# Order of loads and stores at the start of the second SwiGLU product, and the engine of the last scaling

## The chip, the cores and the metric

The kernel runs on one core of a Trainium2 chip. The metric is the device time of one execution in microseconds (us). The core has five engines with a queue each: TensorE (PE; its weight loads are shown apart as PEld), VectorE (DVE), ScalarE (ACT), GpSimd (POOL) and SyncE (SP), which here issues nearly all DMAs, in the order in which the program emits them.

## The reference

One inference step of a two-layer decoder trunk with width 1024, for a prompt of 1024 positions and 8 samples of 4 positions, 1056 columns in all. Layer 0 mixes tokens by sliding-window attention, layer 1 by a recurrent block. After each mixer comes a SwiGLU with 2816 features, and at the end an RMS norm:

```
def swiglu(h, w_in, w_out):
    g, u = jnp.split(h @ w_in, 2, axis=-1)
    return (jax.nn.silu(g) * u) @ w_out

for layer in range(DEPTH):
    ...
    xp = xp + swiglu(rms_norm(xp, ffn_norm[layer]), w_ffn_in[layer], w_ffn_out[layer])
    xs = xs + swiglu(rms_norm(xs, ffn_norm[layer]), w_ffn_in[layer], w_ffn_out[layer])
y_prompt = rms_norm(xp, final_norm)
```

## The kernel before

**Tiles.** The columns lie in three tiles of 384, 384 and 288 (t = 0, 1, 2). A matrix of 1024 rows is held as 8 blocks of 128 partitions. All products are done in three passes, of a high and a low part of each operand (`mm3`, L310): an operand is copied to the high part on ACT, and the low part is a subtraction on DVE.

**First product.** `ffn_phase` goes over 22 blocks of 128 features. The first two are plain. The other 20 go in pairs of items from `blocks(f)`: `seven` does tiles 0 and 1 by a Strassen-like scheme of seven half products per pair of feature blocks (operands B11, B21, B22 of the normed input `xn` and their sums T1 to T4), and `h_in` does tile 2. Each item ends in a `post` that computes the gated features on ACT and DVE and puts them aside in DRAM: `keep` copies a tile to a buffer `hi` (ACT, L891), subtracts it (DVE, L892) and stores both halves (SP, L893 and L894). There is one buffer `hi` of one tag and two of another, `xs`, used in turn; a buffer is free again when its store has landed. An odd block stores six tiles of tiles 0 and 1 (`keep_pair`), then one of tile 2. The residual x had been put aside in DRAM (`xd`) before, for room.

**Second product.** It runs over 5 chunks of 4 feature blocks, 4 units each, `unit(w, ws, o, mp, steps)`. A unit has nine operands per chunk (b11, t3, b21, t2, h0, h1, t4, t1, b22; loaded by `fetch`, L202) and 66 matmuls. Its products go into PSUM banks and are added on DVE to x in SBUF (`add`, L1014); a bank that is accumulated further waits for the add that reads it. `add` is pinned: on DVE it stands behind the instruction emitted just before it. A unit's weights come as one raw tile (`load`, L149; two raw buffers), which `parts` splits (ACT L134, DVE L135) and turns into sums on POOL (L155 to L158), which `sums` splits in turn. Unit u issues the load of unit u + 3 and the parts of unit u + 2; within the units both splits are pinned too.

**The seam.** The work around the last two blocks (`y` for NF - 2, `z` for NF - 1) is written out by hand in `lead`, lists of actions put between the items. In `drive` an item runs its `fn` (the matmuls), frees its buffers, prepares what it can, and then runs its `post` (the stores). Before, six operands are fetched ahead of y, and the reload of x (six half tiles, L965), three operands and the weight of unit 2 follow the post of the first item of z.

**Room.** Operands and x lie in slots: six of a pool `hp` that the T operands use until the last `seven`, and 18 general ones, of which six are free before y.

**Order.** PE and SP run in the order in which the program emits. ACT, DVE and POOL are ordered by a planner, with the order of emission as priority; `high_priority(60)` moves an instruction 60 places ahead.

**The end.** In layer 1, `h_out` adds the last two feature blocks tile by tile (L1026), `square` collects squares (ACT L365, DVE L366), `rms` turns their sum into a factor (PE L373, DVE, POOL L379), `spread` spreads it over the partitions (PE, and a copy on ACT, L399), and `final_steps` scales x and stores it. The scaling is one fused multiply on DVE that reads the factor from PSUM (L1386), or a pre-scaling on ACT (L1396) and a multiply on POOL (L1384). Tile 0 goes by DVE, tile 1 by ACT and POOL, tile 2 by DVE but for blocks 2 and 5.

Of the kernel before, what the change touches and what calls it, by code (L numbers as in the profile page):

```python
# [12 lines left out]
P = 128  # L13
# [16 lines left out]
NT = 3  # L30
# [7 lines left out]
NP0 = 1  # L38
PRI = 60
NSH = 4  # L40

VEC = {}
_o = 0
# [12 lines left out]
class Slots:  # L56
    def __init__(self, names):
        self.free = list(names)
# [149 lines left out]


class Item:  # L210
    def __init__(self, fn, needs=(), frees=None, order=None):
        self.fn, self.needs = fn, list(needs)
        self.order = self.needs if order is None else list(order)
        self.frees = self.needs if frees is None else list(frees)
        self.halves = [self]
# [36 lines left out]
class Kern:  # L252
# [33 lines left out]
    def drive(self, items):  # L286
        need = [w for it in items if isinstance(it, Item) for w in it.order]
        todo = self.todo = []
        for w in need:
            if w not in todo:  # L290
                todo.append(w)
        for it in items:
            if it is GAP:
                continue
            if not isinstance(it, Item):
                it()
            else:
                while any(w.t is None for w in it.needs):
                    assert todo.pop(0).prep(self)
                post = it.fn(*[w.t for w in it.needs])  # L300
                for w in it.frees:
                    w.free(self)
                while todo and todo[0].prep(self):
                    todo.pop(0)
                if post:
                    post()

# [532 lines left out]
    def ffn_phase(self, l, before, after):  # L840
# [116 lines left out]
            if j == 3:  # L957
                self.freeall(self.xt[0] + self.xt[1])

        def reload():  # L960
            for t in range(NT):
                self.xt[t] = [self.act_tile([P, 4, WMAX], F32, "x") for _ in range(2)]
            for i in range(2):
                for t in range(NT):
                    nc.sync.dma_start(self.xt[t][i][0][:, :, :WID[t]], self.xd[t][:, 4 * i:4 * i + 4, :])  # L965


        def seven(wg, wu, ws, f):
# [47 lines left out]
        def h_out(w0, w1, h, t, steps):  # L1016
            W = WID[t]
            ws = (w0, w1)
            for m in range(KB):
                ps = self.bank()  # L1020
                for c in range(2):
                    self.mm3(ps[:, :W], ws[c][:, 0, m * P:(m + 1) * P], ws[c][:, 1, m * P:(m + 1) * P],
                             h[:, c, 0, :W], h[:, c, 1, :W], c == 0, c == 1)
                x = self.xview(t, m)
                with tc.high_priority(PRI):
                    tt(x, ps[:, :W], x, OP.add)  # L1026
                if l == 1 or t < 2:
                    self.square(t, m)
                for fn in steps.get(m, ()):
                    fn()  # L1030

# [56 lines left out]
        def second():  # L1088

            O = [[Operand(lambda c=c, i=i: OD[c, i], WMAX if isinstance(i, str) else WID[2], pools)  # L1090
                  for i in ("b11", "t3", "b21", "t2", 0, 1, "t4", "t1", "b22")] for c in range(NCH)]
            M = [Mixed(I[f"wz{l}"][c, mp]) for c in range(NCH) for mp in range(4)]
            n = len(M)
            M += [Whole(I[f"wd{l}"][k]) for k in range(2)]
            H = [Operand(lambda t=t: HD_[t], WID[t], pools) for t in range(NT)]
            gate = Gate()

            def do(u, what):
                if u < len(M):
                    getattr(M[u], what)(self)  # L1100

            def fetch(c, i, j):
                for o in O[c][i:j]:
                    assert o.prep(self)

            def pin(on):
                self.pinned = on

            lead = [[lambda: fetch(0, 0, 6)], [lambda: do(0, "load")],
                    [lambda: do(0, "parts"), lambda: do(0, "sums"), lambda: do(1, "load")],  # L1110
                    [reload, lambda: fetch(0, 6, 9), lambda: do(1, "parts"), lambda: do(2, "load")], [lambda: pin(True)],
                    [lambda: pin(False)]]
            items = []
            for u in range(n):
                c, mp = divmod(u, 4)

                def s0(u=u, c=c, mp=mp):
                    if mp < 3 and c + 1 < NCH:
                        fetch(c + 1, 3 * mp, 3 * mp + 3)
                    if mp < 3 and c + 1 == NCH:  # L1120
                        assert H[mp].prep(self)
                    do(u + 1, "sums")
                    do(u + 3, "load")
                    gate.open = u == n - 1

                st = (s0, lambda u=u: do(u + 2, "parts"))
                p = [M[u].w, M[u].s]
                items.append(Item(lambda a, b, *y, mp=mp, st=st: unit(a, b, y, mp, st), p + O[c],
                                  p + (O[c] if mp == 3 else []), [gate]))
            w = [x.w for x in M[n:]]  # L1130
            steps = [{}, {2: n0[1:2], 5: n0[3:4]}, {1: n1[1:2], 4: n1[3:4]}]
            last = [Item(lambda a, b, h, t=t: h_out(a, b, h, t, steps[t]), w + [H[t]],
                         (w if t == 2 else []) + [H[t]], [gate]) for t in range(NT)]
            return lead, items, last
# [8 lines left out]
        for f in range(NPL, NF - 2):  # L1143
            L += blocks(f)
        y, z = blocks(NF - 2), blocks(NF - 1)
        L += lead[0] + [y[0]] + lead[1] + [y[1]] + lead[2] + [z[0]] + lead[3] + [z[1]] + lead[4]
        for i, x in enumerate(units):
            if l == 0 and i < DB:
                L.append(lambda b=i: self.caches(b))
            L.append(x)  # L1150
        L += lead[5] + p[:2] + n0[4:] + [p[2]] + n1[4:]
        if l == 0:
            L += [lambda m=m: self.square(2, m) for m in range(KB)]
        return L, leave
# [222 lines left out]
    def final_steps(self, t):  # L1377
        nc = self.nc
        W = WID[t]

        def apply(kb):
            x = self.xview(t, kb)
            if t == 1 or t == 2 and kb in (2, 5):
                nc.gpsimd.tensor_tensor(x, x, self.rs[t][:, :W], OP.mult)  # L1384
            else:
                nc.vector.scalar_tensor_tensor(x, x, self.gcol("final", kb), self.rp[t][:, :W], op0=OP.mult, op1=OP.mult)  # L1386
            step = 1 if t == 2 else 2
            if (kb + 1) % step == 0:
                k0 = kb + 1 - step
                (nc.scalar if t == 2 and kb % 2 else nc.sync).dma_start(self.O[f"y{t}"][:, k0:kb + 1, :], self.xt[t][kb // 4][0][:, k0 % 4:kb % 4 + 1, :W])  # L1390

        def head():
            self.rms(t)
            for kb in {0: (), 1: range(KB), 2: (2, 5)}[t]:
                x = self.xview(t, kb)
                nc.scalar.activation(x, x, AF.Copy, scale=self.gcol("final", kb))  # L1396

        return [GAP, head, GAP, lambda: self.spread(t, False)] + [lambda kb=kb: apply(kb) for kb in range(KB)]
# [130 lines left out]
```

## Time and profile before

| | |
|---|---|
| time, median of 3 runs | 2211.14 us (2208.36 to 2213.12) |
| time of the profiled execution | 2210.95 us |
| its span, first to last instruction | 2208.9 us |
| PE busy | 2133.2 us, 97% |
| DVE busy | 1496.0 us, 68% |
| ACT busy | 1008.7 us, 46% |
| POOL busy | 237.1 us, 11% |
| granted TensorE clock, mean | 0.983 |
| DMA | 310.12 MB, mean 140 GB/s |

A row of the timeline gives the start, the length, the engine, the line of the kernel, the operation, what is written and read (out<-in) and the count, and in brackets the idle time of the engine just before, with what ended it. "SPq" is SP's queue issuing a DMA; a landing time runs from the issue to the last byte. A row of the stretch table gives the stretch, its length, the busy time of PE, PEld, DVE, ACT and POOL with counts, the granted clock, the share of DMA engines busy and GB/s. A busy PE is not PE at its peak.

### The profile page before, as it was taken

To read this page: it belongs to the slowest core of one execution; us is meant where nothing else is said; L and a number is where in the kernel's file an instruction comes from. 1 tells how busy PE (TensorE), PEld (TensorE's weight loads), DVE (VectorE), ACT (ScalarE), POOL (GpSimd) and SP (SyncE) were. 2 spreads that over 40 slices of the span, in tenths; PEclk is the share of its full clock that TensorE was granted. 3 is DMA by queue.
4 is the path that set the end of the run, shared out by engine and by line. 5 is a ranking of instruction groups with operands and counts; after the bars stand their busy time and mean duration, and the time that the engine had idled before them with its cause. 6 is when DMAs were issued, how large, how long until landed. Compare 5 with 4: busy or idle time off the path is not lost.

```text
span 2208.9 us, 35229 instructions
## 1 busy us (share of the span) xinstructions
PE 2133.2 (97%) x13608; PEld 2107.0 (95%) x13608; DVE 1496.0 (68%) x2934; ACT 1008.7 (46%) x1841; POOL 237.1 (11%) x328
## 2 busy tenths in 40 slices
PE   9999999999999997999999989999999999979996
PEld 8899989999999997999999989999999999969996
DVE  6877687756666654666786787787566666546666
ACT  5666665434444442112268886754444444411213
POOL 1224230000000001222100000000000000113222
PEclk9999999999999998999999999999999999989998
DMA  5332425233343356764211123432433433586622
GB/s 191 102 103 80 135 99 176 99 107 124 132 138 127 113 180 265 274 231 184 92 49 58 58 87 115 149 137 80 162 114 121 144 127 122 204 304 229 224 104 79
DMA packets 131632, 310.12 MB, mean 140 GB/s; under 512 B 14152, under 2 KB 84872, under 8 KB 131464
## 3 DMA queue, kind: packets, MB, share of 16 engines
q1 hardware_dynamic: 130128, 306.95, 40.5%
q8 instruction: 107, 1.75, 0.3%
q10 hardware_dynamic: 1336, 0.92, 0.1%
q14 instruction: 61, 0.50, 0.1%
HBM read 223.15 MB, written 86.65 MB: 140 GB/s over the span
## 4 chain that ended last, share of the span: by engine, by line
PE 82%; DVE 8%; ACT 4%; DMA 3%; issue 1%; POOL 1%; SPq 0%; ACTq 0%; DVEq 0%; POOLq 0%
PE mm L310 79%; DMA raw<-in_wz 1%; DVE w L87 1%; PE pt L630 1%; ACT w L83 1%; PE s L582 1%; DVE s L600 1%; ACT s L607 1%; DVE acc L366 1%; DMA x<-xd 1%; DVE xn L349 0%; PE mm L373 0%; DVE pr L349 0%; ACT w L134 0%; DVE xs L425 0%
## 5 line engine op out<-in xcount | busy, mean ns | idle before, releaser
L310 PE MATMUL mm<-xn,w 128*128 128x384 f32 (+1 forms) x5808 | 927.2, 318 | 11.7 <-DVE w L87 3.8
L310 PEld LDWEIGHTS mm<-xn,w 128*128 128x128 f32 x5808 | 900.8, 188 | 18.2 <-DVE w L87 4.7
L310 PE MATMUL mm<-o,w 128*128 128x384 f32 (+1 forms) x2928 | 482.6, 327 | 35.0 <-DVE x L1014 24.6
L310 PEld LDWEIGHTS mm<-o,w 128*128 128x128 f32 x2928 | 478.7, 192 | 36.8 <-DVE x L1014 25.7
L310 PE MATMUL mm<-T,w 128*128 128x384 f32 x1920 | 351.3, 338 | 0.3 <-ACT sg L983 0.3
L310 PEld LDWEIGHTS mm<-T,w 128*128 128x128 f32 x1920 | 338.9, 188 | 0.6 <-ACT sg L983 0.6
L87 DVE TENSOR_TENSOR w<-raw,w 128x1024 fp32r<-128x1024 f32 x202 | 245.4, 1222 | 111.5 <-ACT w L83 110.4
L1014 DVE TENSOR_TENSOR x<-mm,x 128x384 f32<-128x384 f32 x360 | 191.5, 534 | 158.0 <-PE mm L310 143.5
L83 ACT ACTIVATE w<-raw 128x1024 fp32r<-128x1024 f32 x204 | 215.1, 1056 | 131.2 <-PE mm L310 63.3
L134 ACT ACTIVATE w<-raw 128x1024 fp32r<-128x1024 f32 x84 | 85.0, 1053 | 360.4 <-POOL raw L158 299.0
L155 POOL TENSOR_TENSOR raw<-raw 128x256 f32<-128x256 f32 x40 | 29.4, 736 | 1213.8 <-DVE w L135 1213.8
L135 DVE TENSOR_TENSOR w<-raw,w 128x1024 fp32r<-128x1024 f32 x84 | 102.0, 1216 | 41.5 <-ACT w L134 41.5
L622 POOL TENSOR_SCALAR s<-s,sm 128x256 f32<-128x256 f32 (+1 forms) x128 | 84.2, 675 | 207.6 <-DVE sm L620 100.9
L310 PE MATMUL mm<-att,w 128*128 128x384 f32 (+1 forms) x576 | 97.2, 325 | 0.0
L310 PE MATMUL mm<-y,w 128*128 128x384 f32 (+1 forms) x576 | 93.5, 323 | 0.0
L310 PEld LDWEIGHTS mm<-att,w 128*128 128x128 f32 x576 | 91.4, 188 | 1.9
L310 PEld LDWEIGHTS mm<-y,w 128*128 128x128 f32 x576 | 92.4, 188 | 0.0
L607 ACT ACTIVATE s<-s,sm 128x256 f32<-128x256 f32 (+1 forms) x128 | 61.7, 484 | 46.1 <-DVE sm L604 46.0
L891 ACT ACTIVATE hi<-e 128x384 fp32r<-128x384 f32 x80 | 41.8, 523 | 73.1 <-DVE e L1005 33.0
L116 DVE TENSOR_TENSOR w<-raw,w 128x1024 fp32r<-128x1024 f32 x40 | 48.9, 1223 | 36.2 <-ACT w L114 36.1
L365 ACT ACTIVATE sq<-x 128x384 f32<-128x384 f32 (+1 forms) x105 | 50.9, 491 | 38.1 <-DVE x L1026 14.3
L892 DVE TENSOR_TENSOR t<-t,hi 128x384 fp32r<-128x384 f32 x60 | 33.4, 556 | 45.6 <-ACT hi L891 44.4
(208 smaller groups left out, 2284.2 us busy)
## 6 DMA issues: line engine op xcount, KB each, us to landing
o<-od SPq DMA_DIRECT2D x70, 768.0 KB, 7.7
od<-hi SPq DMA_DIRECT2D x140, 192.0 KB, 2.0
raw<-in_wg SPq DMA_DIRECT2D x44, 512.0 KB, 4.1
raw<-in_wu SPq DMA_DIRECT2D x44, 512.0 KB, 4.8
raw<-in_wz SPq DMA_DIRECT2D x40, 512.0 KB, 3.6
od<-e SPq DMA_DIRECT2D x80, 192.0 KB, 2.0
raw<-in_wq SPq DMA_DIRECT2D x24, 512.0 KB, 3.6
raw<-in_wo SPq DMA_DIRECT2D x24, 512.0 KB, 3.6
```

The lines of the kernel that those rows point to most:

```text
L83: nc.scalar.activation(self.t[:, 0, :], raw, AF.Copy)
L87: nc.vector.tensor_tensor(self.t[:, 1, :], raw, self.t[:, 0, :].bitcast(F32), OP.subtract)
L116: tt(d[:, 1, :], g, d[:, 0, :].bitcast(F32), OP.subtract)
L134: pin(nc.scalar.activation(self.t[:, 0, :], raw, AF.Copy))
L135: pin(nc.vector.tensor_tensor(self.t[:, 1, :], raw, self.t[:, 0, :].bitcast(F32), OP.subtract))
L310: mm = lambda *a, **k: self.nc.tensor.matmul(*a, skip_group_check=more, **k)
L365: nc.scalar.activation(sq[:, :W], self.xview(t, kb), AF.Square)
L607: nc.scalar.activation(s[:, j, :N], s[:, j, :N], AF.Exp, bias=sm[:, 1, j:j + 1], accum_out=sm[:, 3, j:j + 1])
L622: nc.gpsimd.tensor_scalar(s[:, j, :N], s[:, j, :N], sm[:, 4, j:j + 1], 1.0, op0=OP.mult, op1=OP.mult)
L891: nc.scalar.activation(hi.bitcast(F32R), src, AF.Copy)
L892: tt(src.bitcast(F32R), src, hi, OP.subtract)
L1014: tc.keep_in_program_order(tt(x, ps[:, :WID[t]], x, OP.add))
```

## The change

Three things. First, `reload` is split in two halves of x (blocks 0 to 3 and 4 to 7 of each tile). The first half of all three tiles and three operands go ahead of y. Second, an `Item` may have actions `mid`, which run after its matmuls and before its `post`: in the first item of z these are the fetch of the other six operands and the second half of x, so SP issues them ahead of that item's stores. The parts of unit 1 and the load of unit 2 stay behind the post. Third, at the end: tile 1 scales blocks 5 and 7 by ACT and POOL and the other six on DVE, and tile 2's squares in `h_out` of layer 1 get priority 60.

```
+POOLED = [(), (5, 7), (2, 5)]
...
+                for f in it.mid:
+                    f()
                 if post:
                     post()
...
-        def reload():
+        def reload(i):
             for t in range(NT):
-                self.xt[t] = [self.act_tile([P, 4, WMAX], F32, "x") for _ in range(2)]
-            for i in range(2):
-                for t in range(NT):
-                    nc.sync.dma_start(self.xt[t][i][0][:, :, :WID[t]], self.xd[t][:, 4 * i:4 * i + 4, :])
+                if i == 0:
+                    self.xt[t] = []
+                self.xt[t].append(self.act_tile([P, 4, WMAX], F32, "x"))
+                nc.sync.dma_start(self.xt[t][i][0][:, :, :WID[t]], self.xd[t][:, 4 * i:4 * i + 4, :])
...
-                    self.square(t, m)
+                    with tc.high_priority(PRI if t == 2 else 0):
+                        self.square(t, m)
...
-            lead = [[lambda: fetch(0, 0, 6)], [lambda: do(0, "load")],
+            lead = [[lambda: reload(0), lambda: fetch(0, 0, 3)], [lambda: do(0, "load")],
                     [lambda: do(0, "parts"), lambda: do(0, "sums"), lambda: do(1, "load")],
-                    [reload, lambda: fetch(0, 6, 9), lambda: do(1, "parts"), lambda: do(2, "load")], [lambda: pin(True)],
-                    [lambda: pin(False)]]
+                    [lambda: fetch(0, 3, 9), lambda: reload(1)], [lambda: do(1, "parts"), lambda: do(2, "load")],
+                    [lambda: pin(True)], [lambda: pin(False)]]
...
-        L += lead[0] + [y[0]] + lead[1] + [y[1]] + lead[2] + [z[0]] + lead[3] + [z[1]] + lead[4]
+        z[0].mid = lead[3]
+        L += lead[0] + [y[0]] + lead[1] + [y[1]] + lead[2] + [z[0]] + lead[4] + [z[1]] + lead[5]
...
-            if t == 1 or t == 2 and kb in (2, 5):
+            if kb in POOLED[t]:
                 nc.gpsimd.tensor_tensor(x, x, self.rs[t][:, :W], OP.mult)
             else:
                 nc.vector.scalar_tensor_tensor(x, x, self.gcol("final", kb), self.rp[t][:, :W], op0=OP.mult, op1=OP.mult)
...
-            for kb in {0: (), 1: range(KB), 2: (2, 5)}[t]:
+            for kb in POOLED[t]:
                 x = self.xview(t, kb)
                 nc.scalar.activation(x, x, AF.Copy, scale=self.gcol("final", kb))
```

More of the change, by code (lines that the diff above doesn't have):

```diff
@@ L210, with __init__ @@
 class Item:
-    def __init__(self, fn, needs=(), frees=None, order=None):
-        self.fn, self.needs = fn, list(needs)
+    def __init__(self, fn, needs=(), frees=None, order=None, mid=()):
+        self.fn, self.needs, self.mid = fn, list(needs), mid
         self.order = self.needs if order is None else list(order)
@@ L1150, in ffn_phase @@
             L.append(x)
-        L += lead[5] + p[:2] + n0[4:] + [p[2]] + n1[4:]
+        L += lead[6] + p[:2] + n0[4:] + [p[2]] + n1[4:]
         if l == 0:
```

## The prediction

> **What bounds the kernel now.** I read the page's table of engines first, then the waits of TensorE (PE) around the places that the change touches, then the timeline there.
>
> ```profile
> PE 2133.2 (97%) x13608; PEld 2107.0 (95%) x13608; DVE 1496.0 (68%) x2934; ACT 1008.7 (46%) x1841; POOL 237.1 (11%) x328
> ```
>
> PE is the bound, so a change pays only where PE stands still or runs at a reduced clock. The change touches the start of the second product in each layer, and the tail. There the waits of PE name two releasers, the adds of L1014 and the transfer o<-od; the timeline of PE has the places, with the idle time before each row in brackets. Layer 0, then layer 1, and one row of the stretch table for the undisturbed product (its length, then PE busy with the count of matmuls):
>
> ```profile
> 856.21 3.33 PE L310 MATMUL mm<-o,w 128*128 128x384 f32 x18
> 868.54 4.78 PE L310 MATMUL mm<-o,w 128*128 128x384 f32 x18 [9.00 <-DVE x L1014]
> 878.45 5.98 PE L310 MATMUL mm<-o,w 128*128 128x384 f32 x24 [5.12 <-DMA o<-od]
> 887.01 6.39 PE L310 MATMUL mm<-o,w 128*128 128x384 f32 x19 [2.58 <-DVE x L1014]
> ```
>
> ```profile
> 1927.64 3.33 PE L310 MATMUL mm<-o,w 128*128 128x384 f32 x18
> 1940.90 4.53 PE L310 MATMUL mm<-o,w 128*128 128x384 f32 x18 [9.92 <-DVE x L1014]
> 1950.74 5.76 PE L310 MATMUL mm<-o,w 128*128 128x384 f32 x24 [5.32 <-DMA o<-od]
> 1959.56 5.61 PE L310 MATMUL mm<-o,w 128*128 128x384 f32 x31 [3.06 <-DVE x L1014]
> ```
>
> ```profile
> 1960.71:2150.11 189.40, 189.40 (x1189) 189.40 (x1189) 124.26 (x198) 37.35 (x37) 50.83 (x69) 1.00 0.53 193
> ```
>
> Layer 0 loses 9.00 + 5.12 + 2.58 = 16.7 us in three stalls, layer 1 18.3 us. One matmul costs 189.40/1189 = 0.159 us on average at full clock. The first unit's 61st matmul (18 + 18 + 24 = 60 before it) should start 9.6 us after the first. It starts 887.01 - 856.21 = 30.8 us after it in layer 0 and 31.9 us in layer 1: 21.2 and 22.3 us are lost by then, more than the stalls, because PE restarts slowly (18 matmuls in 4.78 us where 18 x 0.159 = 2.9). After the third stall the 19 matmuls of layer 0 take 6.39 us instead of 3.0 (3.4 lost), the 31 of layer 1 5.61 instead of 4.9 (0.7). All this, 21.2 + 3.4 + 22.3 + 0.7 = 47.6 us, is the most that the first part of the change can bring.
>
> **The three stalls, from the queues of SP, ACT and DVE (layer 0).**
>
> ```profile
> 852.92 0.32 SPq L893 DMA_DIRECT2D od<-hi  x1
> 858.19 0.40 SPq L893 DMA_DIRECT2D od<-hi  x1
> 859.31 0.52 ACT L891 ACTIVATE hi<-t 128x384 fp32r<-128x384 f32 x1 [1.92 <-DMA od<-hi]
> 860.39 0.44 ACT L891 ACTIVATE hi<-sg 128x288 fp32r<-128x288 f32 x1 [0.56 <-DMA od<-hi]
> 862.37 0.56 DVE L892 TENSOR_TENSOR t<-t,hi 128x384 fp32r<-128x384 f32 x1 [1.04 <-ACT hi L891]
> 863.37 3.49 SPq L965 DMA_DIRECT2D x<-xd  x6
> 866.90 1.60 SPq L202 DMA_DIRECT2D o<-od  x3
> 867.92 0.56 DVE L1014 TENSOR_TENSOR x<-mm,x 128x384 f32<-128x384 f32 x1 [5.00 <-DMA x<-xd]
> 869.80 0.33 SPq L149 DMA_DIRECT2D raw<-in_wz  x1
> 871.25 0.86 SPq L893 DMA_DIRECT2D od<-hi  x1
> 883.34 1.06 ACT L134 ACTIVATE w<-raw 128x1024 fp32r<-128x1024 f32 x1 [21.00 <-DMA raw<-in_wz]
> 884.43 1.23 DVE L135 TENSOR_TENSOR w<-raw,w 128x1024 fp32r<-128x1024 f32 x1 [11.98 <-ACT w L134]
> ```
>
> Stall one: the reload of x stands on SP behind twelve stores of the last block; the first add waits for it until 867.92, PE restarts 0.62 us later. Stall two: t4 is the seventh transfer of the same burst. Stall three: the weight of unit 2 is issued at 869.80 behind the burst; its split on DVE (L135) is pinned in program order ahead of the unit's later adds, so those wait with it. Landing times of single DMAs: the last of the burst (868.05), then the store of 871.25, and the last operand of layer 1 (1940.31):
>
> ```profile
> DMA to landing us min/median/max: 14.0/14.0/14.0
> DMA to landing us min/median/max: 12.5/12.5/12.5
> DMA to landing us min/median/max: 14.4/14.4/14.4
> ```
>
> Sizes and median landing times, from the page's DMA issues:
>
> ```profile
> od<-hi SPq DMA_DIRECT2D x140, 192.0 KB, 2.0
> o<-od SPq DMA_DIRECT2D x70, 768.0 KB, 7.7
> ```
>
> A half x tile is as large as an operand; tile 2's pieces (288 of 384 columns) have 576 KB. The burst (six x, three operands, 7 x 768 + 2 x 576 KB = 6.7 MB) takes 868.05 + 14.0 - 863.37 = 18.7 us. A store takes 2.0 us in the median and 12.5 us behind a burst: **transfers land in the order of issue**. Both facts decide what the change is worth.
>
> **The change part by part.** *Loads moved on SP.* No load is added or removed. Before the block of NF-2 go three half x tiles and b11, t3, b21 in place of six operands (4.5 MB for 4.3 MB; nothing waits there, and 0.2 MB more costs about 0.5 us that the 20 us of matmuls behind them cover). In the last block, ahead of its stores, go t2, h0, h1, t4, t1, b22 and the other three half x tiles: 6.5 MB. Their slots are those of that block's T operands, and the first comes free when the fifth of its seven products has read it:
>
> ```profile
> 843.54 4.39 PE L310 MATMUL mm<-T,w 128*128 128x384 f32 x24
> ```
>
> That is six of these 24 matmuls in, 844.6 us. SP blocks there; behind it stand only stores that are not ready before 852.9. So the burst lands from about 849 to at most 844.6 + 18.7 = 863.3 us, against 882.1 before. t4 is then there before PE asks for it: **stall two goes**. The x halves that units 0 and 1 add to came with the earlier group.
>
> *What takes the place of stall one.* The first add is pinned on DVE behind the split of the last kept tile (hi<-sg, L892). Its hi buffer is one of a few that are reused: the ACT rows above wait for the landing of an earlier store. These stores are issued at 852.9 to 858.2 as before, but now behind the burst: they land after 863.3, not 2.0 us after issue. At 18.7 us for 6.7 MB a store of 0.2 MB takes 0.55 us, and the fifth (the hi store of 858.19, which releases hi<-sg) lands near 863.3 + 5 x 0.55 = 866.1. Then ACT 0.44, DVE 0.46, hand-offs: the first add at about 867.3, or 869 if the scheduler puts the last split (t4's, one more store landing of 2.0 us) ahead of it. Before: 867.92. Ends: 864.5 (only the first store is waited for) and 869.5. I take 867.9, no change. In layer 1, whose burst takes 5.5 + 14.4 = 19.9 us:
>
> ```profile
> 1934.80 3.86 SPq L965 DMA_DIRECT2D x<-xd  x6
> 1938.70 2.04 SPq L202 DMA_DIRECT2D o<-od  x3
> ```
>
> the slot comes free at 844.6 + (1927.64 - 856.21) = 1916.0, the fifth store lands at 1916.0 + 19.9 + 2.8 = 1938.7, the first add is near 1940 and PE near 1940.7, against 1940.90. So stall one keeps its length and changes its cause. Behind the waiting hi on ACT stands the weight copy of unit 1's sums; unit 1 wants it at 868.5 + 9.6 us, so some 8 us of slack cover it.
>
> [...]
>
> *Stall three.* The load of unit 2's weight now follows the last block's stores, at about 869, on a queue that is empty: 3.6 us to land by the page.
>
> ```profile
> raw<-in_wz SPq DMA_DIRECT2D x40, 512.0 KB, 3.6
> ```
>
> So the ACT copy ends near 873.7, the split near 875, and the three adds behind it (0.56 each) near 876.7. PE asks at its 61st matmul, 868.5 + 42 x 0.159 + 1.9 (slow restart, 4.78 - 2.9) = 877.1. It just goes; if all slips, 0 to 2 us stay. I take 0.3 a layer.
>
> Sum: layer 0 887.01 - 877.1 = 9.9, and the 3.4 of slow clock after the third stall: 13.3. Layer 1 1959.56 - (1940.9 + 8.6) = 10.1, and 0.7: 10.8. Together 24.1, less 0.6: **23.5 us**.
>
> *The tail.* Tile 1's final scaling loses six of its eight ScalarE pre-scalings (L1396) and six of eight POOL multiplies, and DVE gains six fused multiplies; the squares of tile 2 go ahead in the planner. PE, DVE and POOL there:
>
> ```profile
> 2187.72 2.61 PE L310 MATMUL mm<-o,w 128*128 128x288 f32 x18
> ```
>
> ```profile
> 2177.60 0.56 DVE L366 TENSOR_TENSOR acc<-acc,sq 128x384 f32<-128x384 f32 x1 [0.32 <-ACT sq L365]
> ...
> 2187.68 1.66 DVE L1386 SCALAR_TENSOR_TENSOR x<-x,vec,mm 128x384 f32<-128x384 f32 x3
> 2192.26 5.55 DVE L366 TENSOR_TENSOR acc<-acc,sq 128x288 f32<-128x288 f32 x5
> ...
> 2202.69 2.64 DVE L1386 SCALAR_TENSOR_TENSOR x<-x,vec,mm 128x288 f32<-128x288 f32 x6 [1.80 <-ACT rs L399]
> ```
>
> ```profile
> 2188.49 9.00 POOL L1384 TENSOR_TENSOR x<-x,rs 128x384 f32<-128x384 f32 x8 [4.11 <-ACT rs L399]
> ```
>
> The last matmul group ends at 2190.33, the last sum of squares at 2197.81, 7.5 us later. While POOL multiplies, a sum takes 5.55/5 = 1.11 us, though narrower than the one of 0.56 before it; DVE's fused multiply, which reads PSUM, keeps 0.55 (1.66/3) beside POOL. Without POOL: add, square and sum at some 0.45 each, hand-offs 0.3, and one or two of the moved multiplies in the way (0.61 each, they can't be interrupted): 2.3 to 2.9 us. Gain 4.6 to 5.2. The moved 6 x 0.61 = 3.7 us must fit into the 4.9 us from the last sum to the first multiply of tile 2 (2202.69 - 2197.81); with what is left of tile 0 up to 1.2 us may run over. Ends -1 and 6; I take **4.5 us**.
>
> **The rivals.** *A: the stores do not hold the adds up* (another order on ACT or DVE, or buffers that come free sooner). Then the first add follows the DVE split that ended at 862.93 and PE restarts at 863.5, 5 us sooner; layer 1 likewise 6 us: 2172. With no stall at all, the ceiling, 47.6 + 4.5: 2159. For: ACT's order is the planner's and may be redrawn. Against: the hi rows above wait on DMA landings even with an idle queue.
>
> *B: the loads do not come early* (SP held up at the slots until the block ends): stalls stay, only the tail gains: 2206. Against: the readers are done at 844.6 to 847.9 by the row of T.
>
> *C: stall three stays in part, or the tail gains nothing* because the moved multiplies stand ahead of the squares (3.7 us): 2187 to 2197.
>
> *D, slower:* the burst ahead of the stores. Each us that it lands later delays the first add of a layer by one, with PE standing. The 28 us of gain are spent when it takes 14 us longer in each layer, 33 instead of 18.7. At the mean rate of the whole run,
>
> ```profile
> DMA packets 131632, 310.12 MB, mean 140 GB/s; under 512 B 14152, under 2 KB 84872, under 8 KB 131464
> ```
>
> it would take 46 us: 27 us later twice, 2183 + 55 = 2238. Against: the same nine transfers took 18.7 and 19.9 us.
>
> **How the numbers follow.** The profiled execution took 2210.95 us (span 2208.9), 0.2 below the median 2211.14. 2210.95 - 23.5 - 4.5 = **2183 us**. My case 0.60 (own range 2175 to 2191), A 0.20, B 0.06, C 0.10, D 0.04. The range of 8 in 10 takes in most of A and C: 2166 to 2197. A measurement of this kernel can tell about 0.2% (4.4 us) from no change. Faster: my case, A, C and half of B, with a margin for what I do not see: 0.91. Same 0.05, slower 0.04.
>
> **What would show it.** Right: x<-xd and o<-od issued on SP before the last block's stores; no wait of PE on o<-od; one stall of 7 to 11 us at each start, released by an add (L1014) that had waited on ACT hi, and this on a store's landing of some 6 to 11 us; no DVE wait of 12 us on L134; sums of 0.45 us in the tail and the last one within 3 us of the last product. Wrong: a stall below 5 us (A), an add after 870 us (D), a second stall at the 61st matmul (C).

## The result, and the profile after

The changed kernel takes 2189.84 us, the median of 4 runs (2188.45 to 2190.83), against 2210.56 us for the kernel before on the same chip (2208.36 to 2213.12). The ratio is 0.9905, with a 95% interval of 0.9888 to 0.9923: 20.7 us faster. Forecast were 2183 us, 28 us faster, with a range of 2166 to 2197. The profiled execution took 2189.78 us, its span 2187.9. In the changed kernel the lines stand a little lower: the matmuls of `mm3` are L313, the adds L1017, the copy to `hi` L894, its subtraction L895, the stores L896 and L897, the loads of a weight L150 and its splits L135 and L136.

The page's table of engines first (busy us, share, instructions), then the largest waits of PE (total us, times, longest).

```profile
PE 2129.7 (97%) x13608; PEld 2104.4 (96%) x13608; DVE 1493.8 (68%) x2940; ACT 1005.4 (46%) x1835; POOL 232.8 (11%) x322
```

```profile
PE mm L313 <- DVE x L1017: 19.8, 4, 9.9
PE mm L376 <- DVE acc L369: 6.7, 3, 3.6
```

The first three rows of the same view before:

```profile
PE mm L310 <- DVE x L1014: 24.6, 4, 9.9
PE mm L310 <- DMA o<-od: 10.4, 2, 5.3
PE mm L373 <- DVE acc L366: 10.0, 3, 7.5
```

The wait for operands (10.4 us) is gone, the wait for the sums of squares fell by 3.3 us, and the wait for the adds fell by only 4.8 us, with its longest one unchanged at 9.9. The timeline of PE at the start of the second product, layer 0 and then layer 1, shows which stalls these are (the 18 matmuls ahead of the first row of each layer start at 857.38 and 1918.86):

```profile
869.38 9.21 PE L313 MATMUL mm<-o,w 128*128 128x384 f32 x42 [8.67 <-DVE x L1017]
879.03 21.15 PE L313 MATMUL mm<-o,w 128*128 128x384 f32 x130 [0.43 <-DVE x L1017]
...
1932.10 8.69 PE L313 MATMUL mm<-o,w 128*128 128x384 f32 x42 [9.90 <-DVE x L1017]
1941.56 43.74 PE L313 MATMUL mm<-o,w 128*128 128x384 f32 x272 [0.77 <-DVE x L1017]
```

Of three stalls a layer (9.00, 5.12, 2.58 and 9.92, 5.32, 3.06 us) the first stays (8.67 and 9.90), the second is gone, and 0.43 and 0.77 of the third are left.

The table of all runs, in us, is worked out from such rows of each kernel's profiled execution: "front" ends where the first matmul of the second product in layer 0 starts; "u0" is unit 0 (66 matmuls) and "u1" unit 1; "close" is what follows the twentieth unit, to the last product of that layer's residual; "tail" is from the last product to the end of the span.

```
kernel                     front   L0 u0   u1  close   L1 u0   u1  close  tail    span
before                    856.21   32.89 12.38 27.02   33.08 10.49 29.73 18.62  2208.95
changed                   857.38   22.82 10.55 29.44   23.86 10.55 29.59 15.33  2187.91
e1_seam_only              855.41   23.59 10.55 27.02   22.76 10.55 28.18 18.64  2187.37
e2_tail_only              855.50   32.62 10.49 29.45   33.08 10.96 29.60 15.32  2205.24
e3_own_hi                 857.42   21.95 11.22 29.42   22.39 11.01 29.61 15.31  2187.06
e4_small_burst            857.97   16.94 16.51 29.43   18.04 15.58 29.61 14.52  2189.79
e5_big_burst              855.96   27.90 10.55 29.46   28.42 10.55 31.19 14.43  2196.54
e6_tail_pri_only          857.19   22.93 10.55 29.42   23.46 10.55 28.18 16.46  2187.88
e7_small_late             855.70   19.47 13.53 29.44   18.62 13.90 29.62 14.38  2183.35
e8_pri_tile2              855.49   22.96 10.55 26.99   23.59 10.55 28.04 15.52  2184.43
e9_weights_first          855.10   22.84 10.55 29.45   23.62 10.55 29.60 14.72  2184.07
e10_own_hi_weights_first  860.16   11.75 12.14 29.43   11.74 14.51 28.05 15.49  2173.52
e11_all                   855.71   11.74 12.21 26.99   11.74 11.48 29.59 15.32  2164.82
```

The stretches left out hardly move: the other 18 units of a layer 189.4 to 191.6 us (189.7 in the changed kernel), and between the layers 808.2 to 811.3. Two things in it move with no edit that touches them, and are noise when single rows are compared: the front, by 5 us from kernel to kernel, and the close of layer 1, which is 28.0 to 28.2 or 29.6 to 29.7, and once 31.2 (e5).

So the 21.0 us of span come from: layer 0's units 0 and 1 -11.9, layer 1's -9.2, the tail -3.3, and layer 0's close **+2.4**, which no step of the forecast had; the rest (front +1.2, stretches -0.2, close of layer 1 -0.1) is noise or near it.

### The profile page after: what moved, and what is told of

Its sections match the earlier page's. It is cut to its first block, busy times and chain, and to the rows that moved or that the text cites. A ratio compares the mean times of both kernels' runs of the same rounds, so it can differ in the third digit from the quotient of the medians.

```text
span 2187.9 us, 35226 instructions
## 1 busy us (share of the span) xinstructions
PE 2129.7 (97%) x13608; PEld 2104.4 (96%) x13608; DVE 1493.8 (68%) x2940; ACT 1005.4 (46%) x1835; POOL 232.8 (11%) x322
## 4 chain that ended last, share of the span: by engine, by line
PE 84%; DVE 7%; ACT 4%; DMA 3%; issue 1%; POOL 0%; SPq 0%; ACTq 0%; DVEq 0%; POOLq 0%
PE mm L313 80%; DVE w L88 1%; PE pt L633 1%; DMA o<-od 1%; ACT w L84 1%; DMA od<-hi 1%; PE s L585 1%; DVE s L603 1%; ACT s L610 1%; DVE xn L352 0%; DVE acc L369 0%; PE mm L376 0%; DVE pr L352 0%; DMA raw<-in_wz 0%; ACT g L1252 0%
## 5 line engine op out<-in xcount | busy, mean ns | idle before, releaser
L313 PE MATMUL mm<-xn,w 128*128 128x384 f32 (+1 forms) x5808 | 927.3, 317 | 10.6 <-DVE w L88 3.8
L313 PEld LDWEIGHTS mm<-xn,w 128*128 128x128 f32 x5808 | 901.5, 188 | 16.5 <-DVE w L88 4.5
L313 PE MATMUL mm<-o,w 128*128 128x384 f32 (+1 forms) x2928 | 478.4, 325 | 19.8 <-DVE x L1017 19.8
L313 PEld LDWEIGHTS mm<-o,w 128*128 128x128 f32 x2928 | 475.2, 191 | 20.9 <-DVE x L1017 20.9
L313 PE MATMUL mm<-T,w 128*128 128x384 f32 x1920 | 351.4, 338 | 0.9 <-ACT sg L986 0.9
L313 PEld LDWEIGHTS mm<-T,w 128*128 128x128 f32 x1920 | 338.8, 188 | 1.4 <-ACT sg L986 1.4
L1017 DVE TENSOR_TENSOR x<-mm,x 128x384 f32<-128x384 f32 x360 | 191.1, 534 | 141.3 <-PE mm L313 140.2
L135 ACT ACTIVATE w<-raw 128x1024 fp32r<-128x1024 f32 x84 | 85.3, 1053 | 328.4 <-POOL raw L159 296.2
L156 POOL TENSOR_TENSOR raw<-raw 128x256 f32<-128x256 f32 x40 | 29.6, 739 | 1191.4 <-DVE w L136 1191.4
L136 DVE TENSOR_TENSOR w<-raw,w 128x1024 fp32r<-128x1024 f32 x84 | 102.7, 1222 | 15.4 <-ACT w L135 15.4
L313 PE MATMUL mm<-att,w 128*128 128x384 f32 (+1 forms) x576 | 97.1, 324 | 0.0
L313 PE MATMUL mm<-y,w 128*128 128x384 f32 (+1 forms) x576 | 93.5, 322 | 0.0
L313 PEld LDWEIGHTS mm<-att,w 128*128 128x128 f32 x576 | 91.3, 188 | 1.9
L313 PEld LDWEIGHTS mm<-y,w 128*128 128x128 f32 x576 | 92.4, 188 | 0.0
L894 ACT ACTIVATE hi<-e 128x384 fp32r<-128x384 f32 x80 | 41.8, 523 | 88.6 <-DVE e L1008 33.4
L992 DVE TENSOR_TENSOR sg<-mm,sg 128x384 f32<-128x384 f32 x40 | 22.2, 555 | 62.0 <-PE mm L313 62.0
```

Of the source, the lines that this page charges most:

```text
L135: pin(nc.scalar.activation(self.t[:, 0, :], raw, AF.Copy))
L136: pin(nc.vector.tensor_tensor(self.t[:, 1, :], raw, self.t[:, 0, :].bitcast(F32), OP.subtract))
L156: tt(d, c, d, OP.add)
L313: mm = lambda *a, **k: self.nc.tensor.matmul(*a, skip_group_check=more, **k)
L894: nc.scalar.activation(hi.bitcast(F32R), src, AF.Copy)
L1017: tc.keep_in_program_order(tt(x, ps[:, :WID[t]], x, OP.add))
```

## The experiments

The forecast rests on the *store theory* of stall one: the burst is early enough, but the last block's stores land behind it, so their `hi` buffers come free late, and with them the copy on ACT, the subtraction on DVE and the first add, which is pinned behind that subtraction. It has two rivals. In the *load theory* PE waits until the burst of loads itself is through. In the *compute theory* ACT and DVE are not done sooner whatever the buffers, and the stores have nothing to do with it. For the tail the question was what brings the gain: moving the multiplies from POOL to DVE (*contention theory*: a sum of squares is slow beside POOL), or only the new order of the squares (*order theory*).

### The parts alone: e1_seam_only, e2_tail_only, e6_tail_pri_only, e8_pri_tile2

Each of these is the changed kernel with one part taken back. The first two split it at its seam:

```
e1_seam_only (tile 1's scaling and the squares as before):
-POOLED = [(), (5, 7), (2, 5)]
+POOLED = [(), tuple(range(8)), (2, 5)]
-                    with tc.high_priority(PRI if t == 2 else 0):
-                        self.square(t, m)
+                    self.square(t, m)

e2_tail_only (loads and stores of the seam in the order before):
-            lead = [[lambda: reload(0), lambda: fetch(0, 0, 3)], [lambda: do(0, "load")],
+            lead = [[lambda: fetch(0, 0, 6)], [lambda: do(0, "load")],
...
-                    [lambda: fetch(0, 3, 9), lambda: reload(1)], [lambda: do(1, "parts"), lambda: do(2, "load")],
+                    [], [lambda: reload(0), lambda: reload(1), lambda: fetch(0, 6, 9), lambda: do(1, "parts"), lambda: do(2, "load")],
```

> The new order of loads alone; tile 1 scales all eight blocks by ACT and POOL as before, and tile 2's squares have no priority. If the two parts of the change add up, this takes what the changed kernel takes plus the tail's share: in its trace the stretch from the last product to the end is 3.2 us shorter than before (15.3 against 18.6), so 2193 to 2194 us. If the tail brings nothing of its own: 2190.

> The new tail alone, with the loads in the order of before. If the parts add up: 2210.6 - 3.2, 2206.5 to 2208 us, and the start of the second product as before (first PE stall 9 to 10 us, then 5 and 3). If the gain is all in the seam: 2210 to 2211.

Measured: the seam alone 2190.64 us (2188.4 to 2192.65), ratio 0.9911 (0.9898 to 0.9925); the tail alone 2208.56 (2206.9 to 2210.68), ratio 0.9992 (0.9983 to 1.0001). The seam brings the whole gain that can be measured, and the tail's part by itself can't be told from no change. The table says why the seam alone came out some 3 us lower than the 2193 to 2194 that were expected: the tail's edit gains 3.3 us in the tail, but every kernel that has its `high_priority(0)` has a close of layer 0 of 29.4 us, and the four that don't (the kernel before among them) one of 27.0.

To see which part of the tail's edit does what:

```
e6_tail_pri_only (the squares' priority stays, the multiplies are back on POOL):
-POOLED = [(), (5, 7), (2, 5)]
+POOLED = [(), tuple(range(8)), (2, 5)]

e8_pri_tile2 (no priority block of 0 places; only tile 2 of layer 1 has one):
-                    with tc.high_priority(PRI if t == 2 else 0):
-                        self.square(t, m)
+                    if l == 1 and t == 2:
+                        with tc.high_priority(PRI):
+                            self.square(t, m)
+                    else:
+                        self.square(t, m)
```

> The changed kernel, but tile 1 scales all eight blocks by ACT and POOL as before; only the priority of tile 2's squares stays in the tail. Contention theory (a sum of squares takes twice as long while POOL multiplies): sums of about 1.1 us remain, the last one 5 to 7 us after the last product, 2191.5 to 2194 us. Order theory (the sums were late because they stood behind other work on DVE): the last sum within 4 us of the last product, 2189 to 2191 us.

> The changed kernel, but only tile 2's squares of layer 1 stand in a priority block; the squares of tiles 0 and 1 and all of layer 0 stand in none (in the change they stand in one of 0 places). In all runs so far with that block layer 0's three closing tiles take 29.4 us from the first product of unit 20 to the last, in before and in the kernel without it 27.0. If the block redraws the planner's order there: 27.0 again and 2187 to 2188 us. If it is something else of the change: 29.4 and 2189 to 2191.

Measured: e6 2189.21 us (2187.81 to 2191.11), ratio 0.9911 (0.9897 to 0.9924), which can't be told from the changed kernel. Both signs of the contention theory came, sums of twice the length and a last sum more than 5 us after the last product, and still the time is that of the order theory: POOL is as busy as before there, but DVE has no multiplies of tile 1 left to do behind the last sum. POOL, DVE and PE of e6:

```profile
2169.98 8.55 POOL L1389 TENSOR_TENSOR x<-x,rs 128x384 f32<-128x384 f32 x8 [2.96 <-ACT rs L402]
2174.84 1.89 DVE L369 TENSOR_TENSOR acc<-acc,sq 128x288 f32<-128x288 f32 x2
2176.79 1.44 PE L376 MATMUL mm<-ones,acc 128*128 128x1 f32 x6 [5.36 <-DVE acc L369]
```

Beside POOL a sum takes 1.89/2 = 0.95 us, and PE waits 5.36 us. The same place in the changed kernel:

```profile
2170.95 2.19 POOL L1389 TENSOR_TENSOR x<-x,rs 128x384 f32<-128x384 f32 x2 [4.32 <-ACT rs L402]
2172.93 0.60 DVE L1391 SCALAR_TENSOR_TENSOR x<-x,vec,mm 128x384 f32<-128x384 f32 x1
...
2173.82 0.60 DVE L1391 SCALAR_TENSOR_TENSOR x<-x,vec,mm 128x384 f32<-128x384 f32 x1
...
2175.08 0.60 DVE L1391 SCALAR_TENSOR_TENSOR x<-x,vec,mm 128x384 f32<-128x384 f32 x1
2175.67 0.46 DVE L369 TENSOR_TENSOR acc<-acc,sq 128x288 f32<-128x288 f32 x1
2176.18 1.44 PE L376 MATMUL mm<-ones,acc 128*128 128x1 f32 x6 [3.61 <-DVE acc L369]
```

With POOL idle a sum takes 0.45 us, as the forecast had it, but three moved multiplies (0.60 each) stand between the sums. What each part brings has to be read between profiles with the same close of layer 1. Close and tail together are 46.8 us in e1 (neither part), 44.6 in e6 (the priority alone) and 43.6 in e8 (both), with a close of 28.0 to 28.2 in each. So the new order of the squares brings 2.2 us and the move to DVE some 1.1. The second can't be told from nothing: the times are 2189.21 and 2189.84, and close and tail together differ by 0.9 us (44.0 to 44.9) among the kernels with the whole edit and a close of 29.6. By the Trainium skill, SBUF — State Buffer, section SBUF: two separate sides, a DVE operation with two SBUF inputs and a GpSimd operation that reads SBUF lock each other out of a shared pair of ports. The rows agree in kind: the sum, with two SBUF inputs, goes from 0.45 to 0.95 us beside POOL, and the multiply of L1391, which reads PSUM, keeps 0.60 beside POOL (in e6 at 2171.60).

e8 took 2186.72 us (2186.3 to 2188.29), ratio 0.9897 (0.9884 to 0.9911), with layer 0's close back at 26.99. DVE and PE at the end of that close in the changed kernel, and the same in e8:

```profile
1100.49 0.61 DVE L428 SCALAR_TENSOR_TENSOR xs<-x,vec,rs 128x384 f32<-128x384 f32 x1
...
1101.38 0.55 DVE L369 TENSOR_TENSOR acc<-acc,sq 128x384 f32<-128x384 f32 x1
1101.98 0.83 PE L376 MATMUL mm<-ones,acc 128*128 128x1 f32 x6 [1.31 <-DVE acc L369]
```

```profile
1098.73 0.55 DVE L369 TENSOR_TENSOR acc<-acc,sq 128x384 f32<-128x384 f32 x1
1099.34 0.83 PE L376 MATMUL mm<-ones,acc 128*128 128x1 f32 x6 [0.42 <-DVE acc L369]
```

In the changed kernel a multiply of the next norm (L428) stands on DVE ahead of the last sum of squares; in e8 it comes behind it, at 1100.28. PE waits 0.9 us longer for the sum (1.31 against 0.42), and the 18 matmuls behind it take 1.0 us longer (3.63 against 2.62). A priority block of 0 places thus changed the order on DVE in a place that it wasn't meant for; e8 shows that it costs the 2.4 us. Why a block of 0 places redraws the planner's order is left open.

### What stall one is: e3_own_hi, e4_small_burst, e5_big_burst, e7_small_late

e3 gives the seven tiles that the last block keeps `hi` buffers of their own, out of eight slices of two general slots that are free there, so that no copy waits for a store (`unspare` gives the slots back).

```
e3_own_hi:
-            hi = self.tmp([P, WMAX], "hi", bufs=1) if T["n"] % 2 else \
-                self.gt.tile([P, WMAX], F32, name=self.nm("hi"), tag="xs", bufs=2)
+            if T.get("own"):
+                hi = T["own"].pop(0)
+            else:
+                hi = self.tmp([P, WMAX], "hi", bufs=1) if T["n"] % 2 else \
+                    self.gt.tile([P, WMAX], F32, name=self.nm("hi"), tag="xs", bufs=2)
...
+        def spare():
+            T["spare"] = [self.act_tile([P, 4, WMAX], F32, "hi") for _ in range(2)]
+            T["own"] = [x[0][:, i, :] for x in T["spare"] for i in range(4)]
...
-                    [lambda: fetch(0, 3, 9), lambda: reload(1)], [lambda: do(1, "parts"), lambda: do(2, "load")],
-                    [lambda: pin(True)], [lambda: pin(False)]]
+                    [lambda: fetch(0, 3, 9), lambda: reload(1), spare], [lambda: do(1, "parts"), lambda: do(2, "load")],
+                    [unspare, lambda: pin(True)], [lambda: pin(False)]]
```

> The changed kernel, but the seven tiles that the last block keeps get hi buffers of their own (slices of two general slots that are free there), so no copy waits for the landing of an earlier store; the loads and stores and their order on SP stay. Store theory (the first add stands behind copies that wait for stores which land behind the burst): the first PE stall falls from 8.7 and 9.9 us to 3.5 to 5 us in both layers, 2178 to 2182 us. Load theory (PE waits until the burst of loads is through): no change, 2189 to 2191, as loads land as before. Compute theory (DVE and ACT are not done sooner whatever the buffers): no change either.

Measured: 2187.80 us (2187.35 to 2188.86), ratio 0.9899 (0.9886 to 0.9913). Both the expected stall and the expected time were missed: the stall fell further than to 3.5 us, and the time by 2 us where some 10 were expected. The chain in the changed kernel comes first (SP, then ACT, then DVE):

```profile
845.96 4.27 SPq L203 DMA_DIRECT2D o<-od  x6
...
855.04 0.32 SPq L896 DMA_DIRECT2D od<-hi  x1
...
860.36 0.32 SPq L896 DMA_DIRECT2D od<-hi  x1
...
866.04 0.52 ACT L894 ACTIVATE hi<-e 128x384 fp32r<-128x384 f32 x1 [9.31 <-DMA od<-hi]
...
867.92 0.44 ACT L894 ACTIVATE hi<-sg 128x288 fp32r<-128x288 f32 x1 [0.44 <-DMA od<-hi]
...
868.40 0.46 DVE L895 TENSOR_TENSOR sg<-sg,hi 128x288 fp32r<-128x288 f32 x1 [0.32 <-ACT hi L894]
868.77 1.48 DVE L1017 TENSOR_TENSOR x<-mm,x 128x384 f32<-128x384 f32 x3
```

ACT waits 9.31 us for a store's landing. By the trace it is the store of 855.04, which thus took some 10.9 us to land, against 2.0 in the median; the copy `hi<-sg` of 867.92 is let go by that of 860.36. The adds follow on DVE behind the subtraction of that last tile, as forecast. In e3 the wait is gone, and PE shows what was behind it (the adds are L1028 there, and in e10 and e11). PE, then SP and ACT:

```profile
861.72 6.55 PE L313 MATMUL mm<-o,w 128*128 128x384 f32 x42 [0.96 <-DVE x L1028]
877.29 17.94 PE L313 MATMUL mm<-o,w 128*128 128x384 f32 x98 [9.02 <-DVE x L1028]
```

```profile
869.47 0.38 SPq L150 DMA_DIRECT2D raw<-in_wz  x1
873.62 1.06 ACT L135 ACTIVATE w<-raw 128x1024 fp32r<-128x1024 f32 x1 [11.98 <-DMA raw<-in_wz]
```

Stall one falls from 8.67 to 0.96 us (in layer 1 from 9.90, also to 0.96), which speaks for the store theory and against both rivals, and 9.02 us come back at the 61st matmul: the adds there stand behind the split of unit 2's weight, whose load is issued only at 869.47, behind the stores. That load had a bound of its own, hidden under stall one. The expectation had left it out.

e4 makes the burst ahead of the stores shorter (the second half of x goes behind them), e5 makes it longer (three operands of the next chunk, 3 x 768 KB = 2.4 MB, go with it), and e7 is e4 with unit 1's parts emitted later, right ahead of unit 0 (SP issues the same DMAs in the same order as in e4):

```
e4_small_burst:
-                    [lambda: fetch(0, 3, 9), lambda: reload(1)], [lambda: do(1, "parts"), lambda: do(2, "load")],
+                    [lambda: fetch(0, 3, 9)], [lambda: do(1, "parts"), lambda: do(2, "load"), lambda: reload(1)],
e5_big_burst (and unit 0 does not fetch these again):
+                    [lambda: fetch(0, 3, 9), lambda: reload(1), lambda: fetch(1, 0, 3)], [lambda: do(1, "parts"), lambda: do(2, "load")],
e7_small_late:
+                    [lambda: fetch(0, 3, 9)], [lambda: do(2, "load"), lambda: reload(1)],
-                    [lambda: pin(True)], [lambda: pin(False)]]
+                    [lambda: do(1, "parts"), lambda: pin(True)], [lambda: pin(False)]]
```

> The changed kernel, but the second half of x is reloaded behind the last block's stores and unit 2's weight, so 4.3 MB instead of 6.5 MB go ahead of the stores. Store theory: the stores land some 6 us sooner, the first PE stall falls to 3.5 to 5 us, 2178 to 2183 us. Load theory: shorter too, by as much. Compute theory: 2189 to 2191. A stall would come back at unit 2 if the second half of x were late; it should land by about 880 us, before unit 2 begins.

> The changed kernel, but the first three operands of chunk 1 (2.4 MB, wanted only by unit 4) are fetched ahead of the last block's stores too, so 8.9 MB instead of 6.5 MB stand ahead of them. Store theory: the stores land about 6.5 us later, the first PE stall grows from 8.7 and 9.9 us to about 15 and 16, and the time to 2201 to 2204 us, though no load that PE needs comes later. Load theory, with the needed loads in front: no change, 2189 to 2191. Compute theory: no change.

> The small burst of e4, and the parts of unit 1 (ACT copy, DVE split, four POOL sums) emitted behind the last item of the first product, so the planner places them after the copies and splits of the last block. If what is left of the first stall is DVE's and ACT's work on that block (3.5 to 5 us), slowed by POOL and by the parts of unit 1, it falls to 1 to 3 us; 2172 to 2179 us. If the parts come too late for unit 1 instead, a stall of up to 5 us appears about 10 us after the start of the product, and the time is that of e4 or above.

PE at the restart in layer 0, e4, e5 and e7 in this order, each with what came next where it stalled again:

```profile
864.71 8.12 PE L313 MATMUL mm<-o,w 128*128 128x384 f32 x42 [3.40 <-DVE x L1017]
889.34 5.97 PE L313 MATMUL mm<-o,w 128*128 128x384 f32 x24 [4.77 <-DVE x L1017]
```

```profile
873.15 9.30 PE L313 MATMUL mm<-o,w 128*128 128x384 f32 x42 [13.86 <-DVE x L1017]
```

```profile
855.70 9.62 PE L313 MATMUL mm<-o,w 128*128 128x384 f32 x60
873.08 12.29 PE L313 MATMUL mm<-o,w 128*128 128x384 f32 x66 [7.76 <-DVE x L1017]
```

e5 took 2199.24 us (2198.35 to 2200.59), ratio 0.9957 (0.9944 to 0.9969): stall one grows by 5.2 us in layer 0 and by 4.5 in layer 1 (14.4) for 2.4 MB more, slightly less than expected (2201 to 2204 us). e4 took 2190.81 (2190.66 to 2191.99), ratio 0.9913 (0.99 to 0.9927): stall one shrinks to 3.4 and 4.4 us. So its length goes with the bytes ahead of the stores in both directions. e4 alone would fit the load theory too, but what e5 adds is wanted only by unit 4; with e3 this settles it for the store theory. But in e4 nothing is gained, where 2178 to 2183 us was expected, because 4.77 us come back in unit 1 (3.83 in layer 1). There the split of unit 3's weight is late; its load and its copy in e4 are

```profile
877.59 0.33 SPq L150 DMA_DIRECT2D raw<-in_wz  x1
885.67 1.06 ACT L135 ACTIVATE w<-raw 128x1024 fp32r<-128x1024 f32 x1 [8.92 <-DMA raw<-in_wz]
```

e7 took 2186.20 (2183.74 to 2189.41), ratio 0.9899 (0.9884 to 0.9914), where 2172 to 2179 was expected. Stall one is gone in it: all 60 matmuls run in a row, though the same stores hold up the copies on ACT as in e4. The first copy that waits on ACT and the first add on DVE in e7:

```profile
859.55 0.53 ACT L894 ACTIVATE hi<-e 128x384 fp32r<-128x384 f32 x1 [3.96 <-DMA od<-hi]
...
857.01 0.54 DVE L1017 TENSOR_TENSOR x<-mm,x 128x384 f32<-128x384 f32 x1
```

In e7 the split of unit 1's weight is emitted between the last kept tile and the first add. The add is then pinned behind that split and no longer behind the tile's subtraction, and it runs ahead of all that waits. So stall one needs two things: stores that land late, and an add that is pinned behind the copies that wait for them. Again a weight is late in e7: 7.76 us at the 61st matmul for unit 2's and 2.17 in unit 1 for unit 3's. Three edits that removed or cut stall one (e3, e4, e7) thus each gave back most or all of it, to a weight load that stood behind stores, reloads or operands on SP.

### Both bounds at once: e9_weights_first, e10_own_hi_weights_first, e11_all

Now there are two bounds to tell apart: the `hi` buffers, and the loads of weights. e9 takes only the second away: unit 2's weight goes into the burst, and each unit's weight load ahead of its fetches. e10 is e9 with e3's buffers, e11 is e10 with e8's priority.

```
e9_weights_first:
-                    [lambda: fetch(0, 3, 9), lambda: reload(1)], [lambda: do(1, "parts"), lambda: do(2, "load")],
+                    [lambda: fetch(0, 3, 9), lambda: do(2, "load"), lambda: reload(1)], [lambda: do(1, "parts")],
...
                 def s0(u=u, c=c, mp=mp):
+                    do(u + 1, "sums")
+                    do(u + 3, "load")
...
-                    do(u + 1, "sums")
-                    do(u + 3, "load")
```

> The changed kernel, but the weight of unit 2 is loaded right behind the six operands, ahead of the second half of x and of the stores, and each unit issues its weight load ahead of the next chunk's operands. The hi buffers stay as they are. Two-bound theory (the first add waits for stores, and right behind it a later add waits for unit 2's weight): the wait on the weight goes, but the first stall stays and grows by the 0.5 MB more ahead of the stores, to 9 to 11 us: 2189 to 2192 us, nothing gained. If the weight alone were the bound: 2180 or below.

> Both: own hi buffers as in e3 and the weights first as in e9. Two-bound theory: the first stall falls to 1 us as in e3 (0.96), and the 9.0 us that e3 then spends before the 61st matmul go too; unit 0 takes 11 to 13 us instead of 22.8 and 23.9 in both layers, 2166 to 2170 us, though e3 alone gained 2 us and e9 is expected to gain none. If a third bound stands behind them (weight of unit 3, late on SP behind the stores): a stall in unit 1 of up to 5 us a layer, 2172 to 2179.

> e10 with the priority block of e8: the effects add, so e10 less 2.4 us, 2164 to 2168 us.

Measured: e9 2187.90 us (2185.89 to 2188.59), ratio 0.99 (0.9886 to 0.9913), where 2189 to 2192 was expected: with the weights early and the stores still holding the buffers, stall one is 10.21 and 10.93 us, stall three is gone, and unit 0 takes the same time as in the changed kernel (22.84 to 22.82). e10 took 2171.18 (2169.41 to 2175.35), ratio 0.9828 (0.9815 to 0.9842): each edit alone brings 2 us, both together 19. That is the mark of two bounds side by side. The 2166 to 2170 us that were expected are missed by 1 us; the third bound that was named there shows as stalls of 1.32 and 2.77 us in unit 1. e11 took 2167.58 (2165.39 to 2169.84), ratio 0.9811 (0.9797 to 0.9824), and beats both kernels, the changed one by some 22 us. Its waits of PE for the adds, and the timeline of PE in both layers:

```profile
PE mm L313 <- DVE x L1028: 4.0, 4, 1.4
```

```profile
860.01 17.09 PE L313 MATMUL mm<-o,w 128*128 128x384 f32 x108 [0.97 <-DVE x L1028]
878.49 21.71 PE L313 MATMUL mm<-o,w 128*128 128x384 f32 x134 [1.39 <-DVE x L1028]
...
1911.27 17.09 PE L313 MATMUL mm<-o,w 128*128 128x384 f32 x108 [0.97 <-DVE x L1028]
1929.03 56.27 PE L313 MATMUL mm<-o,w 128*128 128x384 f32 x349 [0.66 <-DVE x L1028]
```

19.8 us of these waits have become 4.0. Unit 0 takes 11.74 us in both layers, 1.2 more than a unit that waits for nothing (10.5). Of the 23.1 us of span between it and the changed kernel, units 0 give 11.1 and 12.1, units 1 take back 1.7 and 0.9, layer 0's close gives 2.4; the front (1.7 less) and the stretch between the layers (1.7 more) cancel.

## Why the prediction was right, point by point

**The loads go early, stall two goes: right.** SP issues the burst from 845.96 on, ahead of the last block's stores (forecast: 844.6), and PE no longer waits for o<-od.

**Stall one keeps its length and changes its cause: right, and shown.** Forecast was PE's restart at 868.5 us in layer 0; it came at 869.38, with the whole second product 1.17 us later by the front. In layer 1 PE waits 9.90 us against 9.92. The cause was read off the ACT rows and is shown by e3 (buffers of their own, stall gone), e4 and e5 (length goes with the burst's bytes), and the pin by e7. That the length came out the same is due to the size of this burst and nothing else: e4 and e5 move it both ways. Rival A, in which the stores hold nothing up, is out. The burst was to have landed by 863.3. It started at 845.96 instead of 844.6, mostly by the front, and the second of its three pieces of x, issued at 850.78, landed at 850.78 + 13.2 = 864.0. The landing times of the first two pieces:

```profile
DMA to landing us min/median/max: 11.8/12.5/13.2
```

From 845.96 that is 18.0 us with one piece still out, and the store behind the burst had landed by 866.04, when ACT went on: if they landed in order, the burst took 18.0 to 20.1 us where 18.7 was taken.

**Stall three just goes: right.** 0.43 and 0.77 us are left where 0.3 was taken. Unit 2's weight, on SP and then on ACT and DVE in the changed kernel:

```profile
871.16 0.38 SPq L150 DMA_DIRECT2D raw<-in_wz  x1
875.36 1.06 ACT L135 ACTIVATE w<-raw 128x1024 fp32r<-128x1024 f32 x1 [5.38 <-DMA raw<-in_wz]
876.45 1.22 DVE L136 TENSOR_TENSOR w<-raw,w 128x1024 fp32r<-128x1024 f32 x1 [4.13 <-ACT w L135]
```

The load was expected at 869 and the split's end at 875; they were 871.16 and 877.7. So this chain ran only some 2 us later than forecast, and PE, later by the front and by a slower restart, hid it.

**The sum of the seam: 23.5 us forecast, 21.1 measured.** Layer 0 gave 11.9 where 13.0 was expected, layer 1 9.2 where 10.5 was. Of the 2.4 us that are missing, 1.0 are missing by the 61st matmul: the 42 matmuls after the restart took 9.21 and 8.69 us against 8.6 forecast, and the rest of the third stall (0.43 and 0.77) is 0.6 more than taken, while layer 0's restart came 0.3 us earlier behind the first matmul than before. The other 1.4 are a mis-sized term, that of the slow matmuls behind the third stall, taken as 3.4 and 0.7 us. From the 61st matmul to unit 2 the changed kernel gained 2.75 us in layer 0 (14.47 to 11.72) and nothing in layer 1 (11.64 and 11.71). Two rows of the stretch table of the kernel before, layer 0 and layer 1 behind the third stall, say why (the granted clock is the third number from the end):

```profile
887.00:893.00 6.00, 5.99 (x19) 5.99 (x20) 1.44 (x3) 1.28 (x2) 1.73 (x3) 0.50 1.02 423
1961.50:1965.10 3.60, 3.60 (x23) 3.60 (x22) 2.18 (x4) 2.10 (x2) 0.00 (x0) 1.00 1.02 400
```

In layer 1 PE ran at full clock there, and nothing was lost. The forecast compared the length of a row with its count times 0.159 us, but a row is longer than that even at a clock of 1.00: the first 18 matmuls of each layer have 3.33 us, not 2.9.

**The tail: mis-sized, 4.5 us forecast, 3.3 measured.** The step that failed is "one or two of the moved multiplies in the way": three were, and the last sum came 3.6 us after the last product instead of 2.3 to 2.9. And the mechanism behind it was half right: sums do get faster without POOL (0.45 us), but e6 has two thirds of the gain with POOL at work as before, from the order of the squares alone.

**The priority of the squares outside tile 2: the step that was missed.** The forecast spoke of tile 2's squares alone; `high_priority(PRI if t == 2 else 0)` was read as no change for the others. It cost 2.4 us in layer 0's close, shown by e1, e8 and e11, which lack it. This and the two sizes above (2.4 + 2.4 + 1.2 = 6.0) make up most of the 6.8 us between the forecast and the measured time.

**The ceiling.** The forecast named 2159 us for no stall at all and gave rival A 2172, for stores that hold nothing up. e3 shows that A's price was wrong even where its condition is met: the late weight would have left 2187.8. e11, with both bounds gone, came to 2167.58.

## What to carry to other kernels

Before a stall is priced as removed, ask of each of its waiters what it would wait for next, down to the second and third one: here three edits that removed or cut stall one won at most 4 us, and the gain of 19 us came only with the second bound taken away too. Loads that are moved ahead of stores on the same queue delay whatever waits for these stores' buffers by the bytes of the burst: give the buffers of the last stores room of their own, or don't pin the next step's first instruction behind them, and put the small load that gates the next step ahead of the large ones. And of an edit to a planner's priorities, look at the places it leaves nominally unchanged; a block of 0 places was not neutral.

## What the runs showed of the hardware that was not expected

SP had no more than eight DMAs under way: an issue stood until the DMA eight places before it had landed. In the kernel before, SP's issues and then the landing time of the one of 866.90:

```profile
866.90 1.60 SPq L202 DMA_DIRECT2D o<-od  x3
...
878.33 4.10 SPq L202 DMA_DIRECT2D o<-od  x3
```

```profile
o<-od SPq DMA_DIRECT2D x1, 768.0 KB, 11.4
```

The first of the three landed at 866.90 + 11.4 = 878.3, and the issue eight places behind it is that of 878.33. In the changed kernel eight places lie between these two:

```profile
850.27 1.52 SPq L968 DMA_DIRECT2D x<-xd  x3
...
862.16 0.32 SPq L897 DMA_DIRECT2D od<-t  x1
```

The piece of x landed at 850.27 + 11.8 = 862.1, and the store is issued there. So stores behind a burst can be not only landed but issued late. In the whole trace of either kernel no issue comes ahead of the landing of the DMA eight places before it (411 pairs whose landing is on record), while 22 and 16 come ahead of the one seven places before. SP's DMAs signal their landing on eight semaphores in turn, so the limit may belong to the way in which this program's DMAs are counted and not to the queue; no run here tells. Among the DMAs of SP whose landings are on record, none landed ahead of the one issued before it, in either kernel.
